# Sums of tokens one step apart, and one read-back on GpSimd's queue, in a single-core hybrid decoder layer

## The chip, the cores and the metric

The kernel runs on one core of one Trainium2 chip. The metric is device time in microseconds, the median of several runs: for the kernel before, 818.96 us over three runs (818.04 to 819.02). TensorE multiplies matrices, VectorE and ScalarE work element by element, GpSimd is here used for some transfers and small fills, and SyncE issues most of the transfers (DMAs).

## The reference

One decoder layer with 256 tokens and a model width of 2048, all in 32-bit floating point. Cut to what matters here:

```python
h = rmsnorm(x, norm_mix_g)
u = h @ w_in
c_g, b_g, xa, za, q, fl, iv, og, ga, gb = split(u)
ya = b_g * causal_dwconv3(c_g * xa, conv_w) * silu(za)
yb = ...            # chunked gated recurrence from q, fl, iv, og
m = sigmoid(ga) * (ya @ w_a_out) + sigmoid(gb) * (yb @ w_b_out)
x = x + m @ w_o
gate = sigmoid(rmsnorm(x, ple_norm_g) @ w_ple_gate)
x = x + gate * (p @ w_ple_proj)
return rmsnorm(x, final_norm_g)
```

## The kernel before

Products are made on TensorE in three parts: each operand is cut into a high part (a cast on ScalarE, L164, tiles `whi`) and a low part (a subtraction on VectorE, L165, tiles `wlo`), and high x high, high x low and low x high are added up in PSUM (L1032 to L1034). The weights come in chunks of 1 MB from SyncE's queue (`raw`, L150), are cut in two halves of 1024 columns, and each half serves twelve matmuls of 128x512. Four pairs of `whi`/`wlo` buffers are in turn, so the cutting runs up to three halves ahead of TensorE.

The program walks over a list of items, one for each such half. At each item ("position") it cuts the halves that come up, issues the matmuls of this one, loads chunks further ahead, and then takes one step of every epilogue that is active: the epilogues are generators, and each `yield` gives the step back. For an item of kind S two steps are taken.

The four quarters of 512 columns of the two merge gates (`ga`, `gb`) are made in pairs. Pair 0 is made plainly. For pairs 1 to 3 five of the eight chunks (0, 2, 3, 5, 6) are multiplied with seven products in place of eight, a Strassen scheme: these are the items of kind S. Such an item needs sums of weights, made on VectorE (L696) from `sA`, `sB` (loads on SyncE's queue, L141; two buffers each) and `sT` (loads on GpSimd's queue, L157, with a second load that adds onto the first, L158; three buffers). The sums and `sB` are then cut into `thi`/`tlo` (three buffers) and `bhi`/`blo` (one). It needs sums of tokens as well, which are the same for all three pairs: `token_sums` makes them once, in three portions (`TOGETHER`: one, two and two of the five chunks). A portion adds the high and low parts of the activations (L744, into a buffer called `thi`), makes four sums or differences (L754, into a buffer called `tlo`), casts these to the high part `shi` (ScalarE, L756) and subtracts for the low part `slo` (VectorE, L757). It is active from the end of `ga` of pair 0 on, so that its steps lie in the eight items of `gb` of pair 0, the four of the A product and the four of the B product that follow, and then in the first S items of pair 1.

Behind a pair of gates come the products A and B, whose epilogues multiply them with the gates (L764, L776) and add them (L780) to a merged quarter `m`. Quarters 0 to 2 are written to DRAM and read back later (`unpark`). The last quarter (j = 3) is needed at once by the output product O: `turned` writes it to DRAM in four pieces (`turn`, L299), reads it back in the order of features (L310, 512 KB), and three steps later turns it in blocks of 32x32 on VectorE (L303, tile `back`); `put_m` cuts it into `mh` (L769) and `ml` (L770). By then product O of the first block of 512 columns (j = 0) is near its end: only its chunks 6 and 7 use the last quarter, and TensorE's order takes matmuls of the next block's first chunk (which need quarter 0 alone) ahead of the last of them. A scheduler decides where on each engine the transpose, the cut and these matmuls stand among the splits of weights. Loads of `w_o` (three `raw` buffers of a chunk each) and of `x` (`xs`, for the residual, L987) are in SyncE's queue around it.

The scheduler orders instructions engine by engine with costs and due times of its own; between the end of `ga` of pair 0 and the eighth item of the stage behind pair 3, `pinned` holds VectorE and ScalarE to the order in which the program is written.

Of the kernel before, what the change touches and what calls it, by code (L numbers as in the profile page):

```python
# [47 lines left out]
def hybrid_kernel(ctx, tc, xT, x, pT, prm, gfin, masks, w_in, w_a, w_b, w_o, w_pg, w_pp, out):  # L48
    nc = tc.nc
# [27 lines left out]
    def nm(s):  # L77
        uid[0] += 1
        return f"{s}_{uid[0]}"

    def t4(tag="t4", bufs=None):
        bufs = bufs or {"tmp1": 8, "tmp2": 1, "tmp3": 5}[state["tmp"]]
        return pools[state["tmp"]].tile([P, 1024], F32, tag=tag, bufs=bufs, name=nm(tag))
# [76 lines left out]
    def pair_of(pool, n, tags=("whi", "wlo"), width=2 * CW):  # L160
        return tuple(pool.tile([P, width], F32R, tag=tag, bufs=n, name=nm(tag)) for tag in tags)
# [122 lines left out]
    def blocks(ap):  # L284

        return ap.rearrange("p (c b e) -> p c b e", b=4, e=32)

    def spread(ap, t):

        return ap.rearrange("p (b c t e) -> p t c b e", b=4, c=4, t=NT)[:, t]

    def to_dram(src, tag, bufs):
        d = dram.tile([P, 4, T], F32, tag=tag, bufs=bufs, name=nm(tag))
        to = d.rearrange("(b i) a x -> a i b x", b=4)
        for a in range(4):
            nc.sync.dma_start(out=to[a], in_=src[32 * a : 32 * a + 32, :].rearrange("i (b x) -> i b x", b=4))  # L299
        return d  # L300

    def square_turn(dst, src):
        nc.vector.transpose(  # L303
            out=dst.rearrange("p (k a e) -> p a k e", a=4, e=32), in_=src.rearrange("p (a k e) -> p a k e", a=4, e=32)
        )

    def turned(src, lag, dst=None):
        d = to_dram(src, "turn", 3)
        yield
        nc.sync.dma_start(out=src, in_=d.rearrange("p a x -> p (a x)"))  # L310
        for _ in range(lag):
            yield
        dst = t4() if dst is None else dst
        square_turn(dst, src)
        return dst
# [36 lines left out]
    def ep_f(j, psum):  # L352
        fl = t4()
        scaled(psum, fl, True)
        sn = yield from turned(fl, 4)
        sg = t4()
        nc.scalar.activation(out=sg, in_=sn, func=AF.Sigmoid)
# [47 lines left out]
    def ep_q(j, psum):  # L405
        sg, qt = t4(), t4()
        sig(psum, sg)
        plain_times(psum, sg, qt)
        state["qT", j] = yield from turned(qt, 5, t4("qT", 1))
# [15 lines left out]
    def hgrn(j):  # L425
# [194 lines left out]
        for n in range(8):  # L620
            t, h = n // 4, n % 4
            if n == 4:
# [3 lines left out]
                func=AF.Identity, scale=rh[:, n : n + 1],  # L626
            )
        yb = yield from turned(sq, 3)
        for i in range(4):
            k = j * 4 + i  # L630
# [99 lines left out]
    def token_sums():  # L730
        nu = len(SEVEN[1])
        state["S"] = pair_of(pools["st"], 1, ("shi", "slo"), nu * 4 * P)
        state["S"] = tuple(v.rearrange("p (u s t) -> p u s t", u=nu, s=4) for v in state["S"])
        for first, n in TOGETHER:
            for _ in range(3):
                yield
            F, S = (
                pools["st"].tile([P, 2 * CW], F32R, tag=tag, bufs=3, name=nm(tag))[:, : n * 4 * P].bitcast(F32)
                for tag in ("thi", "tlo")
            )  # L740
            c = SEVEN[1][first]
            hi, lo = (v[:, 2 * c : 2 * (c + n), :] for v in state["hT"])
            Fv = F.rearrange("p (k t) -> p k t", t=T)
            nc.vector.tensor_tensor(out=Fv, in0=hi.bitcast(F32), in1=lo.bitcast(F32), op=ALU.add)  # L744
            yield
            Fv = F.rearrange("p (u r b t) -> p u r b t", u=n, r=2, b=2)
            Sv = S.rearrange("p (u s t) -> p u s t", u=n, s=4)
            a11, a12, a21, a22 = Fv[:, :, 0, 0], Fv[:, :, 1, 0], Fv[:, :, 0, 1], Fv[:, :, 1, 1]
            s1, s2, s3, s4 = (Sv[:, :, i] for i in range(4))
            for out, u, v, op in (  # L750
                (s1, a21, a22, ALU.subtract), (s2, s1, a11, ALU.subtract),
                (s3, a11, a21, ALU.subtract), (s4, a12, s2, ALU.add),
            ):
                nc.vector.tensor_tensor(out=out, in0=u, in1=v, op=op)  # L754
            hi, lo = (v[:, first : first + n] for v in state["S"])
            nc.scalar.activation(out=hi, in_=Sv, func=AF.Copy)  # L756
            nc.vector.tensor_tensor(out=lo, in0=Sv, in1=hi.bitcast(F32), op=ALU.subtract)  # L757
            yield
# [8 lines left out]
    def put_m(j, m):  # L767
        hi, lo = (x[:, 4 * j : 4 * j + 4, :].rearrange("p k t -> p (k t)") for x in state["mT"])
        nc.scalar.activation(out=hi, in_=m, func=AF.Copy)  # L769
        nc.vector.tensor_tensor(out=lo, in0=m, in1=hi.bitcast(F32), op=ALU.subtract)  # L770

    def ep_bb(j, psum):
        ga, gb = state["ga"], state["gb"]
        for t in range(NT):
            s = slice(t * CW, (t + 1) * CW)
            nc.vector.tensor_tensor(out=gb[:, s], in0=gb[:, s], in1=psum[t], op=ALU.mult)  # L776
        m = t4()
        for t in range(NT):
            s = slice(t * CW, (t + 1) * CW)
            nc.vector.tensor_tensor(out=spread(m, t), in0=blocks(ga[:, s]), in1=blocks(gb[:, s]), op=ALU.add)  # L780
        if j == 3:
            m = yield from turned(m, 3, back())
            put_m(j, m)
        else:
            state["m", j] = to_dram(m, f"m{j}", 1)
            yield

    def back():
        return pools["back"].tile([P, 1024], F32, tag="back", bufs=5, name=nm("back"))
# [116 lines left out]
    def ep_last(t, halves):  # L906
# [7 lines left out]
    epilogues = {  # L914
        "f": ep_f, "q": ep_q, "iv": ep_iv, "og": ep_og, "c": ep_c, "xa": ep_xa, "za": ep_za, "b": ep_b,
        "ga": ep_ga, "gb": ep_gb, "A": ep_a, "B": ep_bb, "O": ep_o, "PG": ep_pg, "PP": ep_pp,
    }

# [177 lines left out]
    for pos, it in enumerate(items[:last_group]):  # L1096
        mark = len(nc.cur_bb.bb.instructions)
        kind, j, c, last = (it[n] for n in ("kind", "j", "c", "last"))
        _, _, w, g, opname = groups[it["gi"]]
# [77 lines left out]
        if pos == begun:  # L1177
            finish()
            second_part()
            active.append(token_sums())  # L1180
            for _ in range(3):
                add_by_dma()
# [118 lines left out]
```

## Time and profile before

| | |
|---|---|
| median of three runs | 818.96 us (818.04 to 819.02) |
| profiled execution | 818.19 us |
| its span, first to last instruction | 816.1 us |
| TensorE busy | 804.2 us, 99% of the span |
| VectorE busy | 589.0 us, 72% |
| ScalarE busy | 459.1 us, 56% |
| GpSimd busy | 49.2 us, 6%, 57 instructions |
| moved by DMA | 198.52 MB, mean 243 GB/s |

The span begins with the first instruction of the core and ends with its last; the profiled execution took 2.1 us more than that. Times of rows are microseconds from the span's start. In a row of the timeline stand the start, the duration, the engine and line, the operation, output and inputs with their shapes, how many of them are merged in the row, and in brackets how long the engine had been idle before it and what ended that. A matmul of 128x512 shows 0.39 us, but is pipelined: what counts is the distance from one start to the next. "SPq" is SyncE's queue of transfers, where a row's start is the issue, not the landing. In the rows by stretch come the length, then busy time and count of TensorE, of its weight loads, of VectorE, ScalarE and GpSimd, then TensorE's granted clock, the busy share of the DMA engines, and GB/s.

### The profile page before, as it was taken

To read this page: it belongs to the slowest core of one execution; us is meant where nothing else is said; L and a number is where in the kernel's file an instruction comes from. 1 tells how busy PE (TensorE), PEld (TensorE's weight loads), DVE (VectorE), ACT (ScalarE), POOL (GpSimd) and SP (SyncE) were. 2 spreads that over 40 slices of the span, in tenths; PEclk is the share of its full clock that TensorE was granted. 3 is DMA by queue.
4 is the path that set the end of the run, shared out by engine and by line. 5 is a ranking of instruction groups with operands and counts; after the bars stand their busy time and mean duration, and the time that the engine had idled before them with its cause. 6 is when DMAs were issued, how large, how long until landed. Compare 5 with 4: busy or idle time off the path is not lost.

```text
span 816.1 us, 10646 instructions
## 1 busy us (share of the span) xinstructions
PE 804.2 (99%) x4059; PEld 664.6 (81%) x4059; DVE 589.0 (72%) x745; ACT 459.1 (56%) x614; POOL 49.2 (6%) x57
## 2 busy tenths in 40 slices
PE   9999999999999999999999999999999999999995
PEld 6888888888888888888888778888888788888885
DVE  6746588767766498766778988987988756677932
ACT  7576476465555466455545556556554546575623
POOL 1000000001000000012000110110100000001210
PEclk9999999999999999999999999999999999999998
DMA  9988555647867555649975898998944887796702
GB/s 334 396 302 287 198 205 169 235 138 270 253 235 250 198 175 195 206 161 327 350 246 194 243 290 289 291 276 260 278 171 174 299 283 281 250 343 267 275 35 103
DMA packets 52659, 198.52 MB, mean 243 GB/s; under 512 B 6784, under 2 KB 16256, under 8 KB 37888
## 3 DMA queue, kind: packets, MB, share of 16 engines
q1 hardware_dynamic: 45792, 181.07, 63.1%
q0 software_dynamic: 6240, 15.73, 8.3%
q10 hardware_dynamic: 576, 1.05, 0.4%
q8 instruction: 31, 0.51, 0.3%
q14 instruction: 20, 0.16, 0.1%
HBM read 184.19 MB, written 13.63 MB: 242 GB/s over the span
## 4 chain that ended last, share of the span: by engine, by line
PE 85%; DVE 7%; issue 3%; DMA 3%; ACT 2%; POOLq 0%; POOL 0%; DVEq 0%; ACTq 0%
PE g L1033 26%; PE g L1034 26%; PE g L1032 26%; DVE wlo L165 3%; PE s L1033 2%; PE s L1034 2%; PE s L1032 2%; DMA sA<-in_w_in 1%; DMA raw<-in_w_pp 1%; DVE tlo L165 1%; ACT whi L164 1%; DMA raw<-in_w_o 1%; DVE sA L696 1%; PE s L479 1%; DVE back L303 0%
## 5 line engine op out<-in xcount | busy, mean ns | idle before, releaser
L165 DVE TENSOR_TENSOR wlo<-raw,whi 128x1024 fp32r<-128x1024 f32 (+1 forms) x264 | 319.6, 1227 | 157.9 <-ACT whi L164 155.9
L164 ACT ACTIVATE whi<-raw 128x1024 fp32r<-128x1024 f32 (+1 forms) x264 | 272.8, 1049 | 205.0 <-PE g L1034 168.8
L1033 PE MATMUL g<-wlo,xh 128*128 128x512 f32 (+1 forms) x738 | 283.9, 385 | 0.0
L1034 PE MATMUL g<-whi,xl 128*128 128x512 f32 (+1 forms) x738 | 283.6, 385 | 0.0
L1032 PE MATMUL g<-whi,xh 128*128 128x512 f32 (+1 forms) x738 | 283.5, 385 | 0.0
L1033 PEld LDWEIGHTS g<-wlo,xh 128*128 128x128 f32 x738 | 138.7, 188 | 27.7 <-DVE wlo L165 0.3
L1032 PEld LDWEIGHTS g<-whi,xh 128*128 128x128 f32 x738 | 138.7, 188 | 27.4
L1034 PEld LDWEIGHTS g<-whi,xl 128*128 128x128 f32 x738 | 138.7, 188 | 27.4
L1033 PE MATMUL g<-wlo,mh 128*128 128x512 f32 x128 | 49.9, 390 | 0.3 <-DVE wlo L165 0.3
L1032 PE MATMUL g<-whi,mh 128*128 128x512 f32 x128 | 49.7, 389 | 0.0
L1034 PE MATMUL g<-whi,ml 128*128 128x512 f32 x128 | 49.5, 389 | 0.0
L1033 PE MATMUL s<-wlo,xh 128*128 128x512 f32 x84 | 32.7, 390 | 0.0
L1034 PE MATMUL s<-whi,xl 128*128 128x512 f32 x84 | 32.7, 389 | 0.0
L1032 PE MATMUL s<-whi,xh 128*128 128x512 f32 x84 | 32.5, 390 | 0.0
L164 ACT ACTIVATE thi<-sA 128x1024 fp32r<-128x1024 f32 x15 | 15.9, 1062 | 27.6 <-DVE sA L696 24.7
L1033 PEld LDWEIGHTS g<-wlo,mh 128*128 128x128 f32 x128 | 24.0, 188 | 5.7 <-DVE wlo L165 0.7
L1032 PEld LDWEIGHTS g<-whi,mh 128*128 128x128 f32 x128 | 24.0, 188 | 5.1
L1034 PEld LDWEIGHTS g<-whi,ml 128*128 128x128 f32 x128 | 24.0, 188 | 4.9
L1034 PE MATMUL g<-whi,ybTl 128*128 128x512 f32 x64 | 24.9, 389 | 0.0
L1033 PE MATMUL g<-wlo,ybTh 128*128 128x512 f32 x64 | 24.9, 389 | 0.0
L1032 PE MATMUL g<-whi,yaTh 128*128 128x512 f32 x64 | 24.9, 389 | 0.0
L1033 PE MATMUL g<-wlo,yaTh 128*128 128x512 f32 x64 | 24.9, 389 | 0.0
(215 smaller groups left out, 908.4 us busy)
## 6 DMA issues: line engine op xcount, KB each, us to landing
raw<-in_w_in SPq DMA_DIRECT2D x66, 1024.0 KB, 5.0
raw<-in_w_o SPq DMA_DIRECT2D x16, 1024.0 KB, 6.1
raw<-in_w_pg SPq DMA_DIRECT2D x16, 1024.0 KB, 5.6
sT<-in_w_in POOLq DMA_DIRECT2D x30, 512.0 KB, 7.4
raw<-in_w_in SPq DMA_DIRECT2D x28, 512.0 KB, 6.6
raw<-in_w_a SPq DMA_DIRECT2D x8, 1024.0 KB, 6.8
raw<-in_w_b SPq DMA_DIRECT2D x8, 1024.0 KB, 6.7
turn<-t SPq DMA_DIRECT2D x60, 128.0 KB, 3.0
```

What stands on the lines that cost most here:

```text
L164: a = nc.scalar.activation(out=hi, in_=src, func=AF.Copy)
L165: v = nc.vector.tensor_tensor(out=lo, in0=src, in1=hi.bitcast(F32), op=ALU.subtract)
L479: nc.tensor.matmul(out, X[:, 0, h, s], X[:, 1, h, t], start=True, stop=True, tile_position=(0, i * n))
L696: nc.vector.tensor_tensor(out=out, in0=a, in1=b, op=ALU.add)
L1032: nc.tensor.matmul(psum, oh, hi, start=first, stop=False)
L1033: nc.tensor.matmul(psum, oh, lo, start=False, stop=False)
L1034: nc.tensor.matmul(psum, ol, hi, start=False, stop=last)
```

## The change

Two edits. In `token_sums` there were three yields before each portion and one after its addition and one after its subtraction, so five steps from one portion to the next; now there are two yields ahead of all, and one before each portion, so that one step without work lies between the end of a portion and the next portion's addition: three steps from one portion to the next. The first portion stays in its step. And `turned` takes a queue for the read-back; the epilogue of B gives GpSimd's for the last quarter, where it was SyncE's. The four writes stay on SyncE's queue, and the other users of `turned` are unchanged.

```diff
-    def turned(src, lag, dst=None):
+    def turned(src, lag, dst=None, queue=None):
         d = to_dram(src, "turn", 3)
         yield
-        nc.sync.dma_start(out=src, in_=d.rearrange("p a x -> p (a x)"))
+        (queue or nc.sync).dma_start(out=src, in_=d.rearrange("p a x -> p (a x)"))
         for _ in range(lag):
             yield
         dst = t4() if dst is None else dst
...
         state["S"] = tuple(v.rearrange("p (u s t) -> p u s t", u=nu, s=4) for v in state["S"])
+        yield
+        yield
         for first, n in TOGETHER:
-            for _ in range(3):
-                yield
+            yield
             F, S = (
                 pools["st"].tile([P, 2 * CW], F32R, tag=tag, bufs=3, name=nm(tag))[:, : n * 4 * P].bitcast(F32)
                 for tag in ("thi", "tlo")
             )
...
         if j == 3:
-            m = yield from turned(m, 3, back())
+            m = yield from turned(m, 3, back(), nc.gpsimd)
             put_m(j, m)
```

In the changed kernel the lines behind this edit have numbers one higher than before (L744 becomes L745, L776 becomes L777).

## The prediction

> **What bounds the kernel now.** I read the page first: the busy times, then the costliest groups, of which the splits of weights on ScalarE.
>
> ```profile
> span 816.1 us, 10646 instructions
> PE 804.2 (99%) x4059; PEld 664.6 (81%) x4059; DVE 589.0 (72%) x745; ACT 459.1 (56%) x614; POOL 49.2 (6%) x57
> L164 ACT ACTIVATE whi<-raw 128x1024 fp32r<-128x1024 f32 (+1 forms) x264 | 272.8, 1049 | 205.0 <-PE g L1034 168.8
> ```
>
> TensorE is busy for all but 12 us, and ScalarE's splits mostly wait for TensorE to give buffers back (168.8 of 205.0): the feeders run ahead, and an edit is worth only what it gives or takes of TensorE's gaps. Therefore I looked for the gaps, in the busy time by stretches of 20 us:
>
> ```profile
> 460.00:480.00 20.00, 18.86 (x82) 15.03 (x81) 17.78 (x20) 13.01 (x15) 3.55 (x4) 1.00 0.95 287
> 500.00:520.00 20.00, 20.00 (x90) 16.57 (x89) 18.51 (x23) 11.08 (x12) 2.36 (x3) 1.00 1.01 325
> 640.00:660.00 20.00, 19.72 (x88) 15.93 (x87) 14.03 (x13) 9.71 (x12) 0.00 (x0) 1.00 0.89 310
> ```
>
> The first number after the length is TensorE's busy time. The first row is the seven-product stage of gate pair 1, in which the token sums are made; the next is that stage of pair 2, without sums, and loses nothing; the last is the start of the output product's second block. The timeline of TensorE at the first place:
>
> ```profile
> 446.04 0.39 PE L1034 MATMUL s<-bhi,slo 128*128 128x512 f32 x1
> 448.76 0.39 PE L1034 MATMUL s<-whi,xl 128*128 128x512 f32 x1
> 448.99 1.36 PE L1032 MATMUL s<-whi,xh 128*128 128x512 f32 x4
> 450.19 0.42 PE L1033 MATMUL s<-wlo,xh 128*128 128x512 f32 x1
> 461.16 1.05 PE L1032 MATMUL g<-thi,shi 128*128 128x512 f32 x3
> 462.05 0.40 PE L1033 MATMUL g<-tlo,shi 128*128 128x512 f32 x1
> 476.13 0.39 PE L1032 MATMUL s<-bhi,shi 128*128 128x512 f32 x1
> 477.66 0.50 PE L1033 MATMUL s<-blo,shi 128*128 128x512 f32 x1 [1.14 <-DVE blo L165]
> ```
>
> From 446.04 to 448.76 are twelve matmuls: 0.227 us each. What a start lies later than that pace is lost: 450.19 by 0.29 (four steps from 448.99), 462.05 by 0.21 (three from 461.16), 477.66 by 1.30, and about 0.10 in the slower matmul behind that. So this place holds **1.9 us**, and no more than that can be won there.
>
> **The change, part one: the sums of tokens.** No instruction is added or dropped; each portion is one addition (L744), four small operations (L754), a cast on ScalarE (shi) and a subtraction (L757). In the changed kernel as built, VectorE's order has the second portion three splits after the first, and the third three splits after the second; before, the third stood within the first sum unit of pair 1, behind pair 1's first weight split:
>
> ```profile
> 421.09 1.23 DVE L165 TENSOR_TENSOR wlo<-raw,whi 128x1024 fp32r<-128x1024 f32 x1 [1.48 <-ACT whi L164]
> 424.34 1.22 DVE L165 TENSOR_TENSOR wlo<-raw,whi 128x1024 fp32r<-128x1024 f32 x1 [2.02 <-ACT whi L164]
> 437.41 1.23 DVE L165 TENSOR_TENSOR wlo<-sA,whi 128x1024 fp32r<-128x1024 f32 x1 [1.16 <-ACT whi L164]
> 438.55 1.22 DVE L744 TENSOR_TENSOR thi<-xh,xl 128x1024 f32<-128x1024 f32 x1
> 445.03 0.41 DVE L754 TENSOR_TENSOR tlo<-thi 128x256 f32<-128x256 f32 x1
> 447.70 1.23 DVE L757 TENSOR_TENSOR slo<-tlo,shi 128x1024 fp32r<-128x1024 f32 x1 [1.12 <-ACT shi L756]
> ```
>
> From 438.55 on VectorE is the one that is late, and there the third portion takes 1.22 (438.55), 2.67 (445.03 to 447.70, the wait for the cast in it) and 1.23 (447.70): 5.1 us. The chain says how that reaches TensorE:
>
> ```profile
> 462.16 1.23 DVE tlo L165
> 463.40 8.67 DMA sA<-in_w_in
> 477.00 0.61 DVE blo L165
> ```
>
> A late subtraction frees a weight buffer late (462.16), so its refill goes out at 463.40, needs 8.67 us, and the splits behind it end at 477.61, when TensorE had wanted them at 476.36. With the portion gone, that release can come as much as 5.1 us earlier; I count on about 2.9 (an estimate: splits of sums can't run further ahead than their buffers allow, which come back from TensorE every six matmuls or more). 1.9 is needed, so the three losses go: **-1.9 us**. That pair 2 runs the same stage at 20.00 of 20.00 is the row for it. Bounds: if the refill takes a microsecond longer than 8.67, the largest loss stays and 0.5 is won (-0.5); -1.9 is the most.
>
> Where the portion goes, VectorE has 1.48 + 2.02 + 1.16 = 4.66 us of waiting for ScalarE in the rows above, which nearly covers 5.1; the rest, 0.5, comes out of the lead of the splits. That lead is about 5.8 us (four buffers, three of them ahead with 12 matmuls of 0.227 each, less 2.35 for one split on both engines), so I put it at nothing; without that cover it would cost 0.5.
>
> **Part two: the read-back over GpSimd's queue.** The rows at the start of the output product's second block, SyncE's queue first (order of engines, not of time):
>
> ```profile
> 638.74 1.78 SPq L299 DMA_DIRECT2D turn<-t  x4
> 640.62 0.39 SPq L150 DMA_DIRECT2D raw<-in_w_o  x1
> 643.95 0.34 SPq L310 DMA_DIRECT2D t<-turn  x1
> 644.38 1.32 SPq L150 DMA_DIRECT2D raw<-in_w_o  x2
> 647.88 1.22 DVE L165 TENSOR_TENSOR wlo<-raw,whi 128x1024 fp32r<-128x1024 f32 x1 [2.54 <-ACT whi L164]
> 649.02 1.24 DVE L303 STREAM_TRANSPOSE back<-t 128x1024 f32<-128x1024 f32 x1
> 648.27 0.61 PE L1032 MATMUL g<-whi,mh 128*128 128x512 f32 x2
> 649.16 0.50 PE L1033 MATMUL g<-wlo,mh 128*128 128x512 f32 x1 [0.28 <-DVE wlo L165]
> ```
>
> One transfer of 512 KB moves. SyncE no longer waits for the four writes (its 643.95), so the two loads of weights behind it (644.38) can go out earlier; the gap here ends with the split of the load of 640.62, which keeps its place, so that is worth nothing. What changes for TensorE is the order on VectorE. Before, the subtraction wlo (647.88) stood ahead of the transpose (649.02). As built, the changed kernel has the **transpose ahead of that wlo**: VectorE sits on the read-back's landing, and behind it in its queue are the wlo that TensorE wants at 648.72 (two steps after 648.27), the next wlo, and ml. So from now on: landing, 1.24 for the transpose (649.02), 1.28 from the wlo's start to the matmul (647.88 to 649.16), together 2.52.
>
> When does it land? The transfer can start when the last write is in; SyncE reacted at 643.95, and I put GpSimd at 644.1 (a tenth or two for another engine, an estimate). GpSimd's queue has loads of this size, 128 rows of 4 KB, in pairs (L157, then L158, which waits for it):
>
> ```profile
> 442.53 0.59 POOL L157 DMA_DIRECT2D sT<-in_w_in  x1 [65.17 <-DVE tlo L165]
> 447.53 1.17 POOL L158 DMA_DIRECT2D sT<-in_w_in  x1 [4.40 <-DMA sT<-in_w_in]
> 577.41 0.59 POOL L157 DMA_DIRECT2D sT<-in_w_in  x1 [3.98 <-DVE tlo L165]
> 583.61 1.17 POOL L158 DMA_DIRECT2D sT<-in_w_in  x1 [5.61 <-DMA sT<-in_w_in]
> ```
>
> From issue to the waiter's start: 5.00 and 6.20 in the first and last of five such pairs, mean 5.42. I take 5.42: VectorE starts at 649.5, TensorE's matmul at 649.5 + 2.52 = 652.0 instead of 649.16: **+2.9 us**. TensorE's order as built then wants the new mh two matmuls later and ml eleven later; mh is cut on ScalarE beside the wlo, and ml, two subtractions behind on VectorE, is done a tenth before it is wanted, so I add nothing. For bounds, the view of the read-back's own line and then that of the tile sT, minimum, median, maximum:
>
> ```profile
> DMA to landing us min/median/max: 4.0/5.2/7.2
> DMA to landing us min/median/max: 4.6/7.4/19.2
> ```
>
> With 4.0 the matmul comes at 650.6 (+1.5), with 7.4 at 654.0 (+4.9). 19.2 belongs to loads with another one of GpSimd's in front; here its queue is empty (POOL 0.00 in 640:660), so I leave it out. The nearest rows are the five pairs, by size, form and empty queue.
>
> The Trainium skill, "DMA: Bandwidth & Descriptors", section "Anatomy of one DMA — SWDGE (gpsimd) path", fits such a transfer at 2.0 us plus its bytes over 436 GB/s, an estimate of 3.2 us here; by it the matmul would come at 649.8 (+0.7) and the sum would be -1.2. The trace does not agree: no pair is under 4.98, beside loads of weights.
>
> **Sum.** -1.9 + 2.9 = +1.0. The profiled execution took 818.19 (span 816.1 and 2.1 around it), 0.77 under the median of the runs; it would take 819.2, and the median 818.96 + 1.0 = **820.0**.
>
> **The rivals.**
> (1) *Early read-back, or no hold.* With a landing like SyncE's 4.0, -1.9 + 1.5 = -0.4: 818.6. If ScalarE's split of that chunk were what ends last anyway, only the 1.9 is left: 817.1. For it: share of DMA 0.89, not full. Against it: in the five pairs nothing came under 4.98.
> (2) *Slower: the read-back lands late.* Its place is the transpose. Now the two loads of weights go out before or with it instead of behind it, 2 MB on the same DMA engines. At the tile's median of 7.4 the gap grows by 4.9: +3.0, 822.0. It decides from 6.1 us between issue and VectorE's start on, where 1.9 is outweighed by 3.54; 6.20 of the last pair lies there, the other four do not.
> (3) *The clock falls in the longer gap.* From 648.72 to 652.0 TensorE would stand still for 3.3 us. What a still TensorE does shows at the end of the span, the last matmul ending at 807.44, clock in the third column from the right:
>
> ```profile
> 807.00:811.00 4.00, 0.44 (x4) 0.23 (x2) 1.74 (x5) 1.72 (x5) 0.55 (x1) 1.00 0.00 0
> 811.00:816.00 5.00, 0.00 (x0) 0.00 (x0) 0.41 (x1) 0.60 (x1) 0.00 (x0) 0.50 0.57 210
> 1.46 3.60 PE L926 MATMUL s<-warm 128*128 128x512 bf16 x8 [1.46 <-DVE warm L922]
> ```
>
> So it stays whole for 3.5 us of standing still (0.5 only after 811). A gap beyond that, with VectorE starting over 5.6 us after the issue, could meet it; the eight warm-up matmuls took 3.60 us, 0.45 each, so such a stretch would add 8 x (0.45 - 0.227) = 1.8: from +1.2 to +3.0, 822.0.
> The Trainium skill, "TensorE: Matmul & The Clock Gate", section "What's actually happening", halves the clock after one idle window of about 3.4 us that runs free of the work, so a gap of 3.3 never fills one, and one of 5 does so in some executions; the end of the span agrees (3.5).
> (4) *Part one wins little.* If the refill of 463.40 lands as late as before, 0.5 goes and 1.4 stays: -0.5 + 2.9 = +2.4, 821.4. Against it stands pair 2; for it, the DMA share of 0.95 there.
> That the change does not do what it says is ruled out by the order as built: both moves are there.
>
> **How the numbers follow.** A run of this kernel can be told from no change beyond about 0.2%, 1.64 us: 817.3 to 820.6. Forecast (read-back between 4.9 and 6.1, part one whole: 819.4 to 820.6): 0.42, all within. Early (1): 0.15, of which 0.06 within and 0.09 faster. Late (2): 0.23, slower. Clock (3): 0.06, slower. Little won (4): 0.14, 0.10 of it slower, 0.04 within. That makes faster 0.09, same 0.52, slower 0.39. The range goes from 817.2 (part one alone) to 822.2 (late, clock and little won, with 0.2 for a run's scatter): what it leaves out is half of the 0.09, and perhaps 0.12 of a read-back above 7.4 or of two rivals at once.
>
> **What would show it.** Right: no gap of TensorE from 446 to 478, 20.00 in 460:480; VectorE without waiting in 419 to 436; in the stretch around 648 a wait of TensorE for wlo of about 3 us, the transpose ahead of that wlo, and GpSimd's issue near 642 to 644. Wrong: a gap near 476 again, whose chain holds an sA load; a matmul with wlo less than 2 us or more than 4.5 us after the last one with whi there; a clock under 1.00 in 650:660; or a new gap anywhere between 20 and 780.

## The result, and the profile after

| | before | changed |
|---|---|---|
| median of six runs | 817.79 us (816.85 to 819.02) | 824.73 us (824.06 to 825.65) |
| ratio of the changed kernel | | 1.0083, 95% interval 1.0072 to 1.0093 |
| span of the profiled execution | 816.1 us | 822.3 us |

The changed kernel is slower by 6.9 us; 820.0 was predicted, with a range to 822.2. The page of the changed kernel, busy times, then the waits of TensorE:

```profile
PE 804.7 (98%) x4059; PEld 665.7 (81%) x4059; DVE 589.3 (72%) x745; ACT 458.5 (56%) x614; POOL 48.9 (6%) x58
```

```profile
PE g L1034 <- DVE wlo L165: 6.8, 2, 5.5
PE s L927 <- DVE warm L923: 1.5, 1, 1.5
PE g L1033 <- ACT whi L164: 0.6, 1, 0.6
```

The wait for `blo` (1.1) is gone, one wait for `wlo` has grown to 5.5. By stretches of 20 us (columns as before):

```profile
440.00:460.00 20.00, 20.00 (x90) 16.57 (x89) 19.51 (x24) 10.45 (x12) 2.37 (x3) 1.00 0.91 287
460.00:480.00 20.00, 20.00 (x90) 16.57 (x89) 18.28 (x19) 13.11 (x15) 3.55 (x4) 1.00 0.89 257
640.00:660.00 20.00, 13.86 (x54) 10.75 (x53) 7.72 (x7) 4.12 (x4) 0.60 (x1) 0.83 0.80 282
```

The stage of the token sums now loses nothing. The start of the output product's second block loses 6 us of busy time, and its clock reads 0.83. That stretch in the timelines of the changed kernel, one fence for each engine: SyncE's queue, GpSimd, ScalarE, VectorE, TensorE.

```profile
637.36 1.77 SPq L299 DMA_DIRECT2D turn<-t  x4
639.23 5.09 SPq L150 DMA_DIRECT2D raw<-in_w_o  x3
```

```profile
643.45 0.60 POOL L310 DMA_DIRECT2D t<-turn  x1 [59.65 <-DMA turn<-t]
```

```profile
646.55 2.01 ACT L164 ACTIVATE whi<-raw 128x1024 fp32r<-128x1024 f32 x2 [3.84 <-DMA raw<-in_w_o]
```

```profile
651.52 1.25 DVE L303 STREAM_TRANSPOSE back<-t 128x1024 f32<-128x1024 f32 x1 [7.55 <-DMA t<-turn]
652.69 2.32 DVE L165 TENSOR_TENSOR wlo<-raw,whi 128x1024 fp32r<-128x1024 f32 x2
```

```profile
646.66 0.39 PE L1035 MATMUL g<-whi,ml 128*128 128x512 f32 x1
647.66 0.73 PE L1033 MATMUL g<-whi,mh 128*128 128x512 f32 x2 [0.61 <-ACT whi L164]
653.93 0.80 PE L1034 MATMUL g<-wlo,mh 128*128 128x512 f32 x1 [5.54 <-DVE wlo L165]
654.52 0.63 PE L1035 MATMUL g<-whi,ml 128*128 128x512 f32 x1
654.95 0.63 PE L1033 MATMUL g<-whi,mh 128*128 128x512 f32 x1
657.04 0.40 PE L1035 MATMUL g<-whi,ml 128*128 128x512 f32 x1
```

And the chain of waits there:

```profile
638.69 4.00 DMA turn<-t
642.93 0.52 issue
643.45 8.05 DMA t<-turn
```

Read upwards from the matmul of 653.93: it waited for wlo, wlo for the transpose, the transpose for a read-back that took 8.05 us. The three weight loads merged in SyncE's row went out at 639.23, 640.76 and 644.00. The second is the one that moved: it is now 2.7 us ahead of the read-back, where it was 0.4 behind it (644.38). The third is 0.6 behind it, and not earlier than before by TensorE's order, which is here ahead by 1.38 (the writes at 637.36 against 638.74; this load at 645.37 before).

What TensorE lost, at 0.227 us a matmul: 647.66 is 0.8 late, because the weight load that ScalarE needed came late too (its wait of 3.84); 653.93 is 5.8 late after the two matmuls from 647.66; and from 653.93 to 657.04 seven steps took 3.1 instead of 1.6, 1.5 more, nearly all because of the clock:

```profile
647.00:649.00 2.00, 0.79 (x3) 0.30 (x2) 0.00 (x0) 1.55 (x2) 0.00 (x0) 1.00 0.99 414
649.00:651.00 2.00, 0.00 (x0) 0.00 (x0) 0.00 (x0) 0.00 (x0) 0.00 (x0) 0.79 0.98 406
651.00:653.00 2.00, 0.00 (x0) 0.00 (x0) 1.48 (x2) 0.20 (x1) 0.00 (x0) 0.50 0.60 233
655.00:657.00 2.00, 2.00 (x6) 1.62 (x5) 1.15 (x2) 0.00 (x0) 0.00 (x0) 0.51 0.52 78
```

0.8 + 5.8 + 1.5 = 8.1, where the kernel before lost 0.44 + 0.11: +7.6 at this place, and -1.9 at the other. The last but one column, the DMA engines' share, is at 0.98 and more until 651: the read-back ran through full engines. But so it did in the kernel before, where it took 4.0 us:

```profile
645.00:647.00 2.00, 2.00 (x11) 1.65 (x10) 0.34 (x1) 0.21 (x1) 0.00 (x0) 1.00 0.99 354
647.00:649.00 2.00, 1.88 (x9) 1.22 (x7) 1.12 (x1) 1.39 (x2) 0.00 (x0) 1.00 1.04 420
```

So full engines alone are not what makes it late; what differs is which transfers went out ahead of it and beside it.

The two profiled executions differ by 6.2 and not by 5.7, because they also differ where both kernels have the same order. In the changed kernel TensorE waits 1.24 us for a wlo at 390.59, behind another read-back, on SyncE's queue; in the first profile of the kernel before the same matmul comes at 389.92 with next to no wait. The last two experiments look at that.

### The profile page after: what moved, and what is told of

Read it like the earlier page. It is cut to its first block, busy times and chain, and to the rows that moved or that the text cites. A ratio compares the mean times of both kernels' runs of the same rounds, so it can differ in the third digit from the quotient of the medians.

```text
span 822.3 us, 10645 instructions
## 1 busy us (share of the span) xinstructions
PE 804.7 (98%) x4059; PEld 665.7 (81%) x4059; DVE 589.3 (72%) x745; ACT 458.5 (56%) x614; POOL 48.9 (6%) x58
## 4 chain that ended last, share of the span: by engine, by line
PE 68%; issue 22%; DVE 4%; DMA 3%; ACT 2%; POOL 0%; SPq 0%; POOLq 0%
PE g L1034 20%; PE g L1035 19%; PE g L1033 19%; PE s L1035 3%; PE s L1033 3%; PE s L1034 3%; DMA t<-turn 2%; DVE wlo L165 2%; DMA turn<-t 1%; ACT whi L164 0%; PE s L927 0%; DVE back L303 0%; ACT mh L770 0%; POOL rhr L281 0%; SPq L299 0%
```

## The experiments

All ratios are to the kernel before on the same chip, with a 95% interval.

**The two edits one by one.** The first run takes the read-back back to SyncE's queue:

```diff
-            m = yield from turned(m, 3, back(), nc.gpsimd)
+            m = yield from turned(m, 3, back())
```

> The changed kernel with the read-back put back on SyncE's queue: only the portions of the token sums are moved. Theory: the gaps at 449, 461 and 476 go and nothing else moves, -1.9 us, ratio 0.9977, and VectorE has wlo ahead of the transpose as before. Rival (little won): the refill of sA still ends last, a gap of 1.3 stays near 476, -0.5 us, ratio 0.9994.

Measured: 0.9973 (0.9963 to 0.9984), 2.2 us faster. The stretches of that kernel:

```profile
440.00:460.00 20.00, 20.00 (x89) 16.54 (x89) 19.55 (x23) 11.22 (x13) 3.44 (x5) 1.00 0.92 288
460.00:480.00 20.00, 20.00 (x90) 16.57 (x89) 18.27 (x20) 12.35 (x14) 2.71 (x5) 1.00 0.91 275
```

No gap is left there; "little won" falls. The second run is the kernel before with `turned`'s new argument and GpSimd's queue, without the moved sums:

```diff
-            m = yield from turned(m, 3, back())
+            m = yield from turned(m, 3, back(), nc.gpsimd)
```

> The kernel before with the read-back on GpSimd's queue and nothing else. Theory: the whole loss is here, the gap near 648 of 5.8 us beside 0.44, a start 0.8 late ahead of it and 1.3 for matmuls at half the clock: +7.5 to +8 us, ratio 1.0095. Rival (the two edits meet): with the sums unmoved the read-back starts 1.4 us later and lands sooner after its issue, a gap under 4 us and no fall of the clock: +2 to +4 us, ratio under 1.005.

Measured: 1.0088 (1.0071 to 1.0106). The whole loss is the second edit's; with the sums unmoved the read-back took 8.08 us and the wait for wlo was 5.8, in its chain and TensorE's row:

```profile
643.52 8.08 DMA t<-turn
```

```profile
654.03 0.80 PE L1033 MATMUL g<-wlo,mh 128*128 128x512 f32 x1 [5.77 <-DVE wlo L165]
```

The 1.3 us at 477 were missing from this profile, although its order there is that of before.

**Whose fault is the late landing?** Two answers were open: GpSimd's own way of issuing, or the weight loads, which SyncE now issues without waiting for the writes (at 639.23 and 640.76, where before the read-back stood behind the first of them). In the third run SyncE's loads go out as in the changed kernel, but the read-back is on ScalarE's queue, which is idle there:

```diff
-            m = yield from turned(m, 3, back(), nc.gpsimd)
+            m = yield from turned(m, 3, back(), nc.scalar)
```

> The changed kernel with the read-back on ScalarE's queue instead of GpSimd's; orders of TensorE, VectorE and SyncE stay those of the changed kernel. Theory (the read-back is late because the weight loads of SyncE now run ahead of and beside it): it lands again some 8 us after its issue, the gap stays above 4.5 us, the clock falls, ratio to before above 1.006. Rival (GpSimd's own way of issuing is slow): it lands in 4 to 5.2 us as on SyncE's queue, a gap under 3 us, no fall of the clock, ratio under 1.002.

Measured: 1.0071 (1.0054 to 1.0089). Its chain and TensorE's row:

```profile
642.74 8.47 DMA t<-turn
```

```profile
653.64 0.79 PE L1034 MATMUL g<-wlo,mh 128*128 128x512 f32 x1 [6.12 <-DVE wlo L165]
```

8.47 us without GpSimd, with a weight load at 640.76 and the next at 644.02: GpSimd's way of issuing is not needed to make the transfer slow. The fourth run makes SyncE wait for the writes as it did, by a transfer of 16 bytes:

```diff
         (queue or nc.sync).dma_start(out=src, in_=d.rearrange("p a x -> p (a x)"))
+        if queue:
+            nc.sync.dma_start(out=state["pad"][:1, :4], in_=d[0:1, :, 0:1].rearrange("p a x -> p (a x)"))
```

> The changed kernel with one more transfer of 16 bytes on SyncE's queue that reads the four written pieces, so that SyncE waits for them as it did and the next weight loads go out behind that wait; the read-back stays on GpSimd's queue and the transpose ahead of wlo. Theory (contention): the read-back lands in 4.6 to 5.9 us, TensorE's gap is 2.5 to 3.5 us, the clock stays whole, ratio 1.000 to 1.002. Rival (GpSimd's own way is slow): it lands after 7.5 us or more, gap above 5, ratio above 1.006.

Measured: 1.0062 (1.0046 to 1.0077), a miss for the theory as I put it. SyncE's queue, GpSimd and VectorE there:

```profile
642.62 0.71 SPq L313 DMA_DIRECT2D pad<-turn  x1
643.43 0.83 SPq L150 DMA_DIRECT2D raw<-in_w_o  x2
```

```profile
643.23 0.59 POOL L311 DMA_DIRECT2D t<-turn  x1 [60.08 <-DMA turn<-t]
```

```profile
650.25 1.25 DVE L304 STREAM_TRANSPOSE back<-t 128x1024 f32<-128x1024 f32 x1 [6.55 <-DMA t<-turn]
```

The two loads went out from 643.43 on, the first only 0.2 after GpSimd's issue, and the read-back still took 7.0. So this run did not separate the two; the tenth holds the loads back altogether. There the 16 bytes are read from what the read-back has brought, and by a dependence the next weight load follows them:

```diff
+        if queue:
+            state["hold"] = nc.sync.dma_start(out=state["pad"][:1, :4], in_=src[0:1, 0:4])
...
-                nc.sync.dma_start(out=raw, in_=w[g, :, c : c + 2, :])
+                d = nc.sync.dma_start(out=raw, in_=w[g, :, c : c + 2, :])
+                if it["kind"] == "O" and it["j"] == 1 and c == 2:
+                    tc.add_manual_dep(d.ins, state["hold"].ins.name, ...)
```

> The changed kernel with a transfer of 16 bytes on SyncE's queue that reads what the read-back has brought, and the next weight loads put behind it, so that only the load of 640.62 is on its way beside the read-back on GpSimd's queue; wlo stays behind the transpose. Theory (the neighbours make it late): it lands 4.5 to 5.5 us after its issue, TensorE's first gap is 2.5 to 3.5 us; the weight loads come later, which may open other gaps, so the time is not what this run is for (1.000 to 1.006). Rival (GpSimd's own way of issuing is slow): 7 us or more as in the run with SyncE's loads released by the writes.

Measured: 1.0003 (0.9990 to 1.0017). GpSimd, then VectorE:

```profile
642.76 0.59 POOL L316 DMA_DIRECT2D t<-turn  x1 [60.53 <-DMA turn<-t]
```

```profile
646.29 1.25 DVE L309 STREAM_TRANSPOSE back<-t 128x1024 f32<-128x1024 f32 x1 [3.02 <-DMA t<-turn]
```

From issue to the transpose 3.5 us on GpSimd's queue, less than expected, if only one weight load is under way and SyncE sends nothing more until the read-back has landed. So GpSimd's queue is not slow by itself, and the neighbours make the read-back late. That the queue has no part in it beside the neighbours is not shown: in the fourth run it was ahead of both loads by 0.2 us and took 7.0, and in the eighth, below, it took 5.9 us on SyncE's queue, behind a weight load issued 3.3 us ahead of it, against 8 and more on the other two queues.

**What does the order on VectorE cost by itself?** The fifth run leaves GpSimd's late read-back and puts wlo ahead of the transpose again, by five steps of lag instead of three:

```diff
-            m = yield from turned(m, 3, back(), nc.gpsimd)
+            m = yield from turned(m, 5, back(), nc.gpsimd)
```

> The changed kernel with five steps instead of three between the read-back and the transpose; SyncE's loads and GpSimd's read-back as in the changed kernel, but VectorE's order is that of before: wlo ahead of the transpose. Theory (what costs is that the wlo stands behind the late transpose): the read-back lands 8 us after its issue again, TensorE has its twelve matmuls of the chunk first and then stands for 2 to 3 us at the first product with the new mh, no fall of the clock, ratio 1.000 to 1.003. Rival (a read-back this late costs the same in either order): one gap over 4.5 us, the clock falls, ratio above 1.006.

Measured: 1.0046 (1.0029 to 1.0062), between the two. TensorE:

```profile
649.11 0.50 PE L1034 MATMUL g<-wlo,mh 128*128 128x512 f32 x1 [0.53 <-DVE wlo L165]
655.34 0.50 PE L1033 MATMUL g<-whi,mh 128*128 128x512 f32 x1 [3.67 <-ACT mh L770]
```

The chunk's matmuls run as in the kernel before, then TensorE stands at the new mh, since the read-back took 8.59 here. Some 3 us of the loss (1.0083 against 1.0046) are due to the order; the rest stays with the landing, in either order. That the clock fell behind a gap of 3.7 I had not expected. The sixth run is the converse: read-back on SyncE's queue, ahead of the loads, but by a dependence wlo behind the transpose:

```diff
+        if pos == parked + 16:
+            follows(state["splits"][1], state["turned"].ins)
...
-        nc.vector.transpose(
+        state["turned"] = nc.vector.transpose(
...
-            m = yield from turned(m, 3, back(), nc.gpsimd)
+            m = yield from turned(m, 3, back())
```

> The sums of tokens moved, the read-back on SyncE's queue ahead of the weight loads, and by a dependence between the two the transpose ahead of wlo on VectorE: the order of the changed kernel without its late landing. Theory: the read-back lands some 5 us after its issue, TensorE's gap is 2.5 to 3.5 us in place of 0.4, the clock stays whole, ratio 0.999 to 1.002. Rival (the order costs nothing by itself): ratio as in the run with the sums alone, 0.997.

Measured: 1.0004 (0.9994 to 1.0015). SyncE's queue, VectorE, TensorE:

```profile
642.59 0.34 SPq L317 DMA_DIRECT2D t<-turn  x1
643.02 1.18 SPq L150 DMA_DIRECT2D raw<-in_w_o  x2
```

```profile
646.42 1.25 DVE L310 STREAM_TRANSPOSE back<-t 128x1024 f32<-128x1024 f32 x1 [2.58 <-DMA t<-turn]
```

```profile
649.01 0.50 PE L1040 MATMUL g<-whi,mh 128*128 128x512 f32 x1 [1.64 <-ACT mh L777]
```

0.4 us ahead of the two loads the read-back takes 3.8 us. The order then costs 0.31% against the run with the sums alone, 2.5 us (some 1.2 either way): nearly what I had predicted for the whole second edit. By the rows it is less, a wait of 1.6 here against 0.4 in the profile with the sums alone. It is not quite the changed kernel's order: TensorE takes a product with the new mh ahead of the one with wlo here.

**The clock.** TensorE gets something to do in the gap: matmuls into an unused bank, whose result nothing reads.

```diff
+            if kind == "O" and j == 0 and c == 6:
+                spare, prior = bank("s"), state["fed"]
+                for n in range(FILL):
+                    d = nc.tensor.matmul(spare, state[opname][0][:, 0, :P], hi[:, :CW], start=n == 0, stop=n == FILL - 1)
...
```

The lines left out hold these matmuls in their place: each behind the one before it, and the next products behind the last.

> The changed kernel with 20 more matmuls of 128x512 on operands that are there, into an unused bank, in the place where TensorE stands still (4.5 us of work that nothing uses). Theory (the gap lets the clock fall, and half speed behind it costs 1.3 us): the clock stays at 1.00, the matmuls behind the gap start every 0.23 us, the end comes 1.2 to 1.5 us earlier than in the changed kernel, ratio to before 1.006 to 1.007. Rival (the slow matmuls wait for their operands): they stay 0.43 apart, ratio 1.008 or more.

Measured, with 20 of them: 1.0074 (1.0058 to 1.0089). A wait of 2.29 us was left, and the matmuls behind it again start 0.43 apart: the clock fell all the same, and neither theory had that. With 29:

```diff
-FILL = 20
+FILL = 29
```

> As the run with 20 more matmuls, with 29 (6.6 us of work that nothing uses), so that TensorE stands still for less than 0.6 us before the late wlo. Theory (the clock falls at the end of a stretch of some 3.4 us in which TensorE stood still for most of it, 2 us and more, not after 3.5 us without a break): the clock stays at 1.00 in 650:660, the matmuls behind the wait start every 0.23 us, the end comes about 1.3 us earlier than in the changed kernel, ratio to before 1.006 to 1.007. Rival (the fall has another cause, such as the burst of transfers): the clock falls again for 3.4 us, ratio 1.0074 or more.

Measured: 1.0078 (1.0055 to 1.0101). The clock stays whole:

```profile
646.00:650.00 4.00, 4.00 (x19) 3.32 (x18) 0.00 (x0) 1.61 (x2) 0.00 (x0) 1.00 1.02 406
650.00:654.00 4.00, 3.35 (x15) 2.44 (x13) 2.29 (x3) 1.01 (x1) 0.00 (x0) 1.00 0.47 184
654.00:658.00 4.00, 2.35 (x9) 1.65 (x10) 2.33 (x3) 0.05 (x1) 0.00 (x0) 1.00 0.45 127
```

The mean granted clock says the same of all executions: 0.996 or 0.997 in the four of this run, 0.993 in all six of the changed kernel. So it is the standing still that lets it fall. But no time came back: the scheduler here took the products with the new mh and ml first, and TensorE waited for those (busy 2.35 of the last 4 us). The price of 1.5 for the clock is therefore read off the rows of the changed kernel, not shown by a run. The four executions with 20 matmuls point the same way, but are few: two with a mean clock of 0.995 took 824.2 and 824.6 us, two with 0.996 and 0.998 took 823.9 and 822.5.

**A version faster than both kernels.** On top of the sums alone, the addition of the last quarter comes one step later, so that VectorE cuts a weight half first and SyncE has a weight load ahead of the four writes:

```diff
+        if j == 3:
+            yield
         m = t4()
```

> The sums of tokens moved, the read-back on SyncE's queue, and the last quarter's addition one step later, so that VectorE cuts the next weight half first: SyncE then has the next weight load ahead of the four writes, and TensorE's order takes 24 and more matmuls of the next block ahead of the first with the new mh. Theory (at this place the gap of 0.4 us hangs on the weight load behind the writes, not on the read-back): the gap near 648 goes, 0.4 to 0.5 us below the run with the sums alone, ratio 0.996 to 0.997. Rival (the read-back, now behind a weight load, comes too late for mh): a gap of over 1 us, ratio above 0.998.

Measured: 0.9972 (0.9962 to 0.9983), not to be told from the sums alone (0.9973) in time, but the gap is gone:

```profile
640.00:660.00 20.00, 20.00 (x90) 16.57 (x89) 11.98 (x11) 8.48 (x9) 0.00 (x0) 1.00 0.91 318
```

TensorE's order there has the first product with the new mh far behind the next block's first chunks, so the read-back's landing ends no wait of TensorE any more.

**Chance or change?** Both kernels once more, unchanged:

> The kernel before, unchanged, profiled a second time. Two gaps are in question: 1.3 us at 477 (there in the first profile, not in the run with the read-back's queue alone, whose order is the same there) and 0.1 to 1.6 us at 389, where every kernel of this study has the same order. Theory (both hang on how long one transfer takes among others and differ from execution to execution): the gap at 477 lies anywhere from 0 to 1.4, that at 389 anywhere from 0.1 to 1.6. Rival (they belong to the kernels): 1.3 again at 477, under 0.3 at 389.

> The changed kernel, unchanged, profiled a second time. Theory: no gap from 446 to 478; the gap at 389 anywhere from 0.1 to 1.6; the read-back near 643 lands after 7.5 to 8.6 us and the wait before wlo is 5 to 6 us again. Rival (the gap at 389 comes with the change): over 1.2 at 389.

The kernel before, again (816.5 us of span):

```profile
390.53 0.50 PE L1033 MATMUL g<-wlo,xh 128*128 128x512 f32 x1 [0.84 <-DVE wlo L165]
477.85 0.50 PE L1033 MATMUL s<-blo,shi 128*128 128x512 f32 x1 [0.71 <-DVE blo L165]
```

A wait of 0.8 at 390.53 without the change, and 0.7 at 477.85 where it had been 1.14: both hang on transfers that differ from execution to execution. In the changed kernel's second profile (824.1 us) there was no gap from 446 to 478, and the wait before wlo was 6.5, somewhat more than expected. Its wait near 390 was 1.30, above the 1.2 that I had named as the sign that this gap comes with the change. The other runs speak against that: the tenth, which has both edits, lost nothing in 380 to 400, the third and the fifth 1.2 and 1.4.

## Why the prediction was wrong

**Part one was right.** -1.9 was predicted, -2.2 measured for it alone. The gaps at 449, 461 and 476 went by the way described; the refill's issue moved from 463.40 to 461.05, and as TensorE itself is 0.67 later there, by 3.0 in its order, where I counted on about 2.9. One sign that I had named did not come: VectorE still waited in 419 to 436 (busy 13.4 of 17 us, 12.3 before), but TensorE lost nothing by it. Not seen beforehand: the largest of these gaps is not the same in every execution (1.30, 0.87, and none in the run with the queue alone), so one profile does not give its mean, and that the size fits so well is in part luck.

**Part two had the right mechanism and the wrong size.** The transpose stands ahead of wlo, and 2.41 us pass from its start to the matmul (651.52 to 653.93; 2.52 predicted). The term that was mis-sized is the read-back: 5.42 us from issue to VectorE's start, taken from five loads on GpSimd's queue; measured were 8.07 (643.45 to 651.52), and 8.1 to 8.6 in every run in which one weight load had gone out 2 to 2.7 us ahead of it and the next followed within 1.3. I had written that the two loads "can go out earlier", and that this "is worth nothing". One of them did go out earlier, by 2.2 us in TensorE's order. That is worth nothing to TensorE, and it costs the read-back 3 to 4.5 us, since this takes 3.5 with the loads held back, and 3.8 to 5.1 ahead of them on SyncE's queue (3.8 in the sixth run, 4.0 in the kernel before, 5.1 in the first run). The five rows were the wrong neighbours to price from: the same size and form, but without two loads of 1 MB issued within 3 us of them. With 8.07 the sum would have been -1.9 + 5.5 = +3.6 before the clock, and the rival "lands late" was the case that came, beyond the 7.4 that I gave it.

A smaller term was short as well: I put GpSimd a tenth or two behind SyncE. It issued the read-back 0.76 us after the last write had landed (638.69 + 4.00 to 643.45), where SyncE took 0.15 in the first run (637.93 + 4.17 to 642.25): 0.6 between the two.

The same loads hit each other: the one that both orders have behind the writes, which I said "keeps its place", took longer as well (7.2 us, 6.1 before), so that ScalarE's cut and TensorE's 647.66 came 0.8 late. That was not in the sum, but it cost nothing on top, as TensorE then waited for the read-back anyway: in the third run this matmul came on time (646.91), and the wait for wlo was longer instead (6.12).

**The clock was the third miss.** I took from the end of the span that TensorE may stand still for 3.5 us. In the changed kernel the clock fell at about 650.2 (0.79 over 649 to 651 is 0.84 us at half), 2 us after the last matmul. Its rival had 0.06, and came together with the late landing. In the profiled execution of the tenth run it fell although the wait was 1.9; TensorE's row and the stretches there:

```profile
648.70 0.69 PE L1042 MATMUL g<-wlo,mh 128*128 128x512 f32 x1 [1.89 <-DVE wlo L170]
```

```profile
648.00:650.00 2.00, 1.30 (x3) 1.06 (x4) 2.00 (x3) 0.63 (x1) 0.00 (x0) 0.71 0.94 299
650.00:652.00 2.00, 2.00 (x6) 1.57 (x5) 0.91 (x1) 0.00 (x0) 0.00 (x0) 0.50 1.03 434
652.00:654.00 2.00, 2.00 (x9) 1.59 (x9) 0.00 (x0) 0.00 (x0) 0.00 (x0) 0.94 0.95 378
```

0.71, 0.50 and 0.94 make 1.16 + 2.00 + 0.24 = 3.4 us at half, from 648.84 on, when TensorE had already resumed. The Trainium skill, "TensorE: Matmul & The Clock Gate", section "What's actually happening", has a free-running window of about 3.4 us, of which one idle lets the clock fall. The length agrees with these rows; that it must be idle from end to end, as I had read it, does not: no wait here but one of 1.9 us lies ahead of the fall, so some 1.5 us of 3.4 were busy. Nor does such a wait always do it: the mean granted clock was 0.995 in this execution, and 0.997 or 0.998 in seven of the run's nine others, as in the kernel before.

**What stays open.** How much of the 1.5 us the clock really costs, since the run that kept it whole had another order on TensorE. And why, in the fourth run, a load issued 0.2 us behind GpSimd's transfer landed ahead of it (5.9 us after its own issue, at 649.3), while on SyncE's queue 0.4 us were enough to keep the read-back at 3.8. That GpSimd's transfer begins later after its issue would explain it, and so would a rival that no run here tests: that transfers of one queue are served in their order, while those of two queues share the engines.

## What to carry to other kernels

A transfer that waits in a queue also holds back what stands behind it; who takes it to another queue releases those transfers, and has to price them against it, not only count what they gain. A latency is priced from rows with the same traffic around them, and an instruction that waits for a landing should not stand ahead of work for TensorE that is ready. If a gap comes near 2 us, count the clock into its price as a chance.

## What the runs showed of the hardware that was not expected

The same 512 KB read-back took 3.5 us on GpSimd's queue with the next loads held back (tenth run) and 3.8 on SyncE's queue ahead of them (sixth). With one 1 MB load issued 2 to 2.7 us ahead of it and another within 1.3 us behind, it took 8.05 (GpSimd's queue), 8.47 (ScalarE's) and 8.59 (GpSimd's, fifth run): its place among megabyte loads mattered by a factor of about two. With both loads 0.2 us and more behind it, it still took 7.0 on GpSimd's queue (fourth run).

In the profiled executions the clock fell to half for 3.4 us after waits of 1.9 us (tenth run), 2.3 (20 more matmuls) and 3.7 (fifth run), and for 6.8 us in the changed kernel (650.2 to 657.0). It did not fall in the sixth run's, whose longest wait was 1.64, nor with 29 more matmuls, where two waits of 0.75 and 1.55 stood less than a microsecond apart. One of the sixth run's nine other executions has a mean clock of 0.994, though, so 1.64 is no safe bound.

GpSimd issued the transfer 0.76 us after the last write had landed (638.69 + 4.00 to 643.45), SyncE 0.15 after (first run).
